# Turning queries by pairs of heads, a two-bank room for scores, and the root's small steps on GpSimd in a two-layer decoder trunk

## The chip, the cores and the metric

The kernel runs on one core of one Trainium2 chip. Its engines are TensorE (PE in the profile, with its weight loads as PEld), VectorE (DVE), ScalarE (ACT), GpSimd (POOL) and SyncE (SP), which issues DMAs. The metric is the device time of one execution in microseconds; lower is better.

## What is computed

A decoder trunk of two layers over 1024 tokens of width 1024 in f32. Layer 0 mixes tokens with a gated short convolution, layer 1 with attention in a sliding window of 128; each is followed by a SwiGLU channel mixer of width 2816. Every sub-layer has an RMS norm before it and a residual sum behind it. The change touches layer 1's attention alone:

```python
qkv = h @ w_qkv                        # 16 query heads, 4 key and 4 value heads, 64 wide
q = rmsnorm(q, q_gain); k = rmsnorm(k, k_gain)          # per head
scores = einsum(q, k) * scale + alibi  # blocks of 128 queries against 256 keys
scores = where(mask, scores, -inf)     # causal, distance below 128
p = softmax(concat([scores, sink]))[..., :-1]
out = einsum(p, v) @ w_o
```

## The kernel before

**Precision.** A f32 product is made of three fast matmuls: each operand is split into hi (the value rounded to the fast format, fp32r) and lo (the rest), and hi x hi, hi x lo and lo x hi are summed in PSUM. "Splitting" is therefore a pair of instructions everywhere: a copy to fp32r on ScalarE (…_hi) and a difference on VectorE or GpSimd (…_lo).

**The order.** From the first channel mixer on, the kernel is one long line written out by hand. `line.work(n, f)` appends n matmuls to TensorE's sequence and moves the plan's clock on by n x 0.2265 us; `at(t, f)` puts other work at a time of that clock. The times only set the order of instructions in each engine's queue; on the chip each engine runs its queue in order and waits by semaphores.

**Attention.** Work goes by m (16 half-tiles of queries: block m // 2 of 128 tokens, half m % 2 of the 16 heads) and by u (32 steps: a half-tile and one of its two key groups g, which share four query heads).

- `lead_in` makes keys, values and queries of the first blocks; then `unit(u)` is called for each step. In a step TensorE does the scores of u, the values of u-2, one piece of fill, the turns (128x128 transposes) of the probabilities of u-1, and five more pieces. A piece is three matmuls: of a coming query tile (`q_piece`), of coming keys and values (`kv_piece`), or, in the last steps, of the product with w_o (`tail_piece`).
- Queries: `q_square`, `q_sum` (sum of squares per head, and `mean_rows`), `q_guess` (Ln and Exp on ScalarE, for 1/sqrt), `q_newton` (one Newton step on VectorE), `q_scale` (q times that root, to SBUF). Then `q_hi` on ScalarE and `q_lo` on GpSimd split q in SBUF into [hi | lo] of each head, 128 columns a head; `q_turn` turns four heads for each g, and `q_keep` copies them out of PSUM. A turned block has hi of one head in partitions 0 to 63, lo in 64 to 127. Keys go the same way (`kv_square` to `kv_scale`, `key_turn`, `key_hi`, `key_lo`), with the key doubled along the partitions.
- Scores of a step lie in two PSUM banks of their own tags: `merge` puts the two halves of a window together, `bias` adds the distances (VectorE, once for each bank), `sink` (GpSimd) writes the sink's column beside them, `least` reduces, `exponents` (ScalarE), `inverse`, `normal` (GpSimd, division), `turn`, `turn_hi`, `turn_lo`, `select` (GpSimd, a triangular mask that splits the window), `values`, `o_copy`, `o_add`, `o_hi`, `o_lo` (GpSimd).
- PSUM has eight banks: P0 to P3 and acc0 to acc3. Query and key products use P0, P1 and P2, all turns of queries and nearly all of keys P3, probabilities' turns and values one acc bank each, scores the other two.
- In the last steps GpSimd also makes the lo part of w_o's first five tiles (line 1010) and issues stores of X (line 1064).

Of the kernel before, what the change touches and what calls it, by code (L numbers as in the profile page):

```python
# [15 lines left out]
P = 128  # L16
D = 1024
T = 1024
# [52 lines left out]
def trunk_kernel(ctx: ExitStack, tc: tile.TileContext, xT, small, table, w_in, w_out, w_kv, w_q, w_o, w_gu, w_dn, out):  # L71
# [13 lines left out]

    def bank(tag):
        uid[0] += 1
        if tag == "acc":
            tag = acc_tags[0]
            acc_tags.rotate(-1)  # L90
        return pm.tile([P, 512], F32, tag=tag, name=f"{tag}_{uid[0]}", bufs=1)
# [1405 lines left out]
    def attention_layer(line, mixer):  # L1497
# [3 lines left out]
        sc_tags = [acc_tags[0], acc_tags[1]]  # L1501
        pt_tag, pv_tag = acc_tags[2], acc_tags[3]
# [110 lines left out]

        def q_piece(m, k):
            c = slice((m % 2) * HALF, (m % 2 + 1) * HALF)
            piece(get_bank(q_ps, m, f"P{m // 2 % 2}" if m % 2 else "P2"), m // 2, k, lambda: (WQ[k][0][:, c], WQ[k][1][:, c]))


        def mean_rows(d, b, n):
            d["m"] = slot("at_m", (P, 8), bufs=2)[:, 0:n]  # L1620
            dve.tensor_scalar(d["m"], d["ss"], 1.0 / HD, tok["eps"][:, b : b + 1], ALU.mult, ALU.add)

        def log_rows(d, n):
            d["y"] = slot("at_y", (P, 8), bufs=2)[:, 0:n]
            act.activation(d["y"], d["m"], AF.Ln)

        def guess_rows(d):
# [49 lines left out]
        def kv_sum(b):  # L1677
            KV[b]["ss"] = slot("at_s", (P, 8), bufs=2)[:, 0:NKV]
            dve.tensor_reduce(KV[b]["ss"], KV[b]["sq"], mybir.AxisListType.X, ALU.add)
            mean_rows(KV[b], b, NKV)  # L1680

        def kv_guess(b):
            log_rows(KV[b], NKV)
            guess_rows(KV[b])

        def kv_scale(b):
            newton_rows(KV[b], NKV)
            y = KV[b]["y"].unsqueeze(2).to_broadcast([P, NKV, HD])
            for e in (0, 1):
                dve.tensor_tensor(kd_room()[:, :, e, :], kv_heads(b, 0), y, ALU.mult)  # L1690
# [8 lines left out]
        def key_turn(b, c):  # L1699
            ps = KT[b, c] = bank(pv_tag if b == 0 and c else "P3")  # L1700
            for g in (0, 1):
                k = kd_room()[:, 2 * c + g].rearrange("p e d -> p (e d)")
                pe.transpose(ps[:, g * P : (g + 1) * P], k, ident)
# [36 lines left out]
        def q_sum(m):  # L1740
            QC[m]["ss"] = slot("at_s", (P, 8), bufs=2)
            dve.tensor_reduce(QC[m]["ss"], QC[m]["x"], mybir.AxisListType.X, ALU.add)
            mean_rows(QC[m], m // 2, 8)

        def q_guess(m):
            log_rows(QC[m], 8)
            guess_rows(QC[m])
# [8 lines left out]
        def q_hi(m):  # L1756
            QC[m]["split"] = slot("G3", (P, 8, 2, HD))
            QC[m]["r"] = QC[m]["split"].bitcast(F32R)
            act.copy(QC[m]["r"][:, :, 0, :], QC[m]["q"])

        def q_lo(m):
            s = QC[m]["split"]
            pool.tensor_tensor(s[:, :, 1, :], QC[m]["q"], s[:, :, 0, :], ALU.subtract)

        def q_turn(m, g):
            ps = QC[m]["ps"] = bank(pt_tag if m == 0 and g else "P3")
            s = QC[m]["split"]
            for i in range(QUAD):
                pe.transpose(ps[:, i * P : (i + 1) * P], s[:, QUAD * g + i].rearrange("p e d -> p (e d)"), ident)

        def q_keep(m, g):
            if g == 0:
                Q[m] = slot(f"G{4 + m % 2}", (P, 2, QUAD * P), F32R)
            act.copy(Q[m][:, g], QC[m]["ps"])
# [16 lines left out]
        def scores(u):  # L1791
            b, c, g = parts(u)
            kz = key_rooms(c)[:, g]
            S[u] = {"ps": [bank(t) for t in sc_tags]}
            for i in range(QUAD):
                q = Q[2 * b + c][:, g, i * P : (i + 1) * P]
                ps = S[u]["ps"][i // 2][:, (i % 2) * 256 : (i % 2) * 256 + 256]
                for e in (0, 1):
                    k = kz[:, e].rearrange("p s j -> p (s j)")
                    if b == 0:  # L1800
                        ps, k = ps[:, 0:P], k[:, 0:P]
                    pe.matmul(ps, q, k, start=e == 0, stop=e == 1)  # L1802

        def logits(u, j):
            b, _, _ = parts(u)
            ps = S[u]["ps"][j].rearrange("p (i s c) -> p i s c", i=2, s=2)
            own_, prev = ps[:, :, b % 2, :], ps[:, :, (b + 1) % 2, :]
            return own_, prev

        def merge(u, j):  # L1810
            o, p = logits(u, j)
            dve.copy_predicated(p, own.unsqueeze(1).to_broadcast([P, 2, P]), o)

        def bias(u, j):
            b, c, g = parts(u)
            o, p = logits(u, j)
            h = 8 * c + QUAD * g + 2 * j
            e = e_room(u)
            dve.tensor_tensor(e[:, 2 * j : 2 * j + 2, 0:P], o if b == 0 else p, room["T"][:, h : h + 2, :], ALU.add)
# [102 lines left out]
        def lead_in(tail_part, tail_item):  # L1922
# [4 lines left out]
            for b in (0, 1):  # L1927
                d = t + (-0.6, 0.1)[b]
                at(d, kv_v_hi, b)
                at(d + 0.5, kv_v_lo, b)  # L1930
                at(d + 1.0, kv_square, b)
                at(d + 1.5, kv_sum, b)
                at(d + 2.2, kv_guess, b)
                at(d + (2.9, 8.2)[b], kv_scale, b)

            def quick(m, t):
                for d, f in (
                    (0.05, q_square),
                    (0.7, q_sum),
                    (1.6, q_guess),  # L1940
                    (2.3, q_newton),
                    (3.1, q_scale),
                    (3.9, q_hi),
                    (4.6, q_lo),
# [12 lines left out]
            def turn_query(m, g, t=None):  # L1957
                line.work(4 * small_turn, q_turn, m, g)
                at(line.end + 0.05 if t is None else t, q_keep, m, g)

            for k in range(NK):
                q_piece(1, k)
                if k in (1, 2):
                    turn_keys(0, k - 1, None, None)
            quick(1, line.end)
            q_piece(2, 0)
            q_piece(2, 1)
            turn_query(0, 0)
            q_piece(2, 2)
            q_piece(2, 3)  # L1970
            turn_query(0, 1)


# [27 lines left out]
            def unit(u, last):  # L2001
# [14 lines left out]
                if u < NU:  # L2016
                    line.work(8 * (small_mm + (0.12 if b else 0.0)), scores, u)
                    e = line.end
                    at(s + 0.3, sink, u)
                    for j in (0, 1):  # L2020
                        if b:
                            at(e + 0.05 + 0.85 * j, merge, u, j)
                        at(e + 0.5 + 0.85 * j, bias, u, j)
                    if b == 0:
                        at(e + 1.5, blank, u)
                    at(e + 1.8, least, u)
                    at(e + 2.65, exponents, u)
                    at(e + 4.75, inverse, u)
                    at(e + 5.0, normal, u)
                    if g == 0:  # L2030
                        kb = (b, 1) if c == 0 else (b + 1, 0)
                        if 0 < kb[0] < NB:
                            turn_keys(*kb, e + 0.3, e + 2.4)
                if 0 <= u - 2 < NU:
# [3 lines left out]
                    at(max(line.end + 0.7, s + 3.6), o_add, u - 2)  # L2038
                    if g == 1:
                        at(s + 6.95, o_hi, n - 1)  # L2040
                        at(s + 7.9, o_lo, n - 1)
                for _ in range(3 if u == NU else 1):
                    next_piece()
                if 0 <= u - 1 < NU:
                    line.work(4 * small_turn, turn, u - 1)
                    at(line.end + 0.05, turn_hi, u - 1)
                    at(max(line.end + 0.7, s + 4.2), turn_lo, u - 1)
                    if u - 1 >= 4:
                        at(line.end + 0.75, select, u - 1, 0)
                        at(max(line.end + 1.4, s + 4.95), select, u - 1, 1)  # L2050
# [4 lines left out]
                for i in range(5):  # L2055
                    next_piece()
                    if i == (1 if g == 0 else 0) and n + 1 < 16:
                        turn_query(n + 1, g, s + 5.8)
                if n + 2 < 16 and g == 0:
                    m = n + 2  # L2060
                    for d, f in (
                        (5.75, q_square),
                        (6.35, q_sum),
                        (7.2, q_guess),
                        (6.8 + 3.4, q_newton),
                        (6.8 + 5.2, q_scale),
                        (6.8 + 6.2, q_hi),
                        (6.8 + 7.3, q_lo),
                    ):
                        at(s + d, f, m)  # L2070
                if g == 1 and n < 12 and n % 2:
                    kb = n // 2 + 2
                    for d, f in (
                        (3.57, kv_v_hi),
                        (5.0, kv_v_lo),
                        (6.0, kv_square),
                        (6.5, kv_sum),
                        (7.2, kv_guess),
                        (6.8 + 3.5, kv_scale),
# [12 lines left out]
            for u in range(NU + 2):  # L2092
# [3 lines left out]
                unit(u, u == NU + 1)  # L2096
            while tails:
# [117 lines left out]
```

## Time and profile before

| | |
|---|---|
| median of 3 runs | 1919.74 us (1919.67 to 1920.07) |
| the profiled execution | 1919.71 us, its span 1918.0 us |
| granted TensorE clock | 1.000 |
| TensorE busy | 1906.7 us, 99% |
| VectorE, ScalarE, GpSimd busy | 1380.0, 855.6, 292.1 us |
| first to last scores of attention | 990.3 to 1209.7 us |

The span is from the first to the last instruction of the profiled execution; its own time has 1.7 us around that. Attention, with its lead-in, is about an eighth of the span, so 1% of the whole is some 8% of it.

### The profile page before, as it was taken

The numbers are of one execution on the slowest core, as the hardware profiler recorded it, in microseconds if no ns is written. First come the engines' busy times: TensorE is split into PE (matmuls) and PEld (weight loads), VectorE is DVE, ScalarE is ACT, GpSimd is POOL, SyncE is SP. The second block draws the span as 40 slices with busy tenths as digits, with TensorE's granted clock in tenths as the row PEclk, the third lists the DMA queues.
The fourth block names the chain that finished last, engine by engine and source line by source line (L and its number), as shares of the span: only waits on it lengthen the run. The fifth ranks groups of instructions, "written<-read, shape, count | busy, mean of one in ns | idle before, by whom it ended". The sixth has DMA issues, their size and how long they took to land.

```text
span 1918.0 us, 24702 instructions
## 1 busy us (share of the span) xinstructions
PE 1906.7 (99%) x8681; PEld 1579.5 (82%) x8681; DVE 1380.0 (72%) x2352; ACT 855.6 (45%) x1703; POOL 292.1 (15%) x462
## 2 busy tenths in 40 slices
PE   9999999999999999999999999999999999999999
PEld 8888888888888888888888887788888888888887
DVE  8997877867676767765768887678767776765543
ACT  5543444533333334444656766446333333344441
POOL 0000011011111111000015667500111111110000
PEclk9999999999999999999999999999999999999999
DMA  8522176145556447996710003433445555477563
GB/s 314 172 99 75 64 286 223 61 159 198 172 179 209 166 142 265 328 320 222 235 62 1 1 23 132 146 119 116 163 169 180 205 172 177 152 276 275 199 226 102
DMA packets 146765, 325.29 MB, mean 170 GB/s; under 512 B 14288, under 2 KB 54352, under 8 KB 146512
## 3 DMA queue, kind: packets, MB, share of 16 engines
q1 hardware_dynamic: 122592, 239.26, 36.9%
q0 software_dynamic: 23904, 84.42, 12.2%
q8 instruction: 68, 1.11, 0.2%
q14 instruction: 57, 0.47, 0.1%
q10 hardware_dynamic: 144, 0.03, 0.0%
HBM read 228.76 MB, written 94.90 MB: 169 GB/s over the span
## 4 chain that ended last, share of the span: by engine, by line
PE 92%; DVE 3%; issue 1%; POOL 1%; ACT 1%; DMA 1%; SPq 0%; POOLq 0%; DVEq 0%; ACTq 0%
PE acc L920 16%; PE acc L921 16%; PE acc L923 16%; PE P L920 9%; PE P L921 9%; PE P L923 9%; PE acc L1039 2%; PE acc L1037 2%; PE acc L1038 2%; PE P L1599 2%; PE P L1597 2%; PE P L1598 2%; PE acc L158 1%; PE acc L1802 1%; PE acc L1888 1%
## 5 line engine op out<-in xcount | busy, mean ns | idle before, releaser
L920 PE MATMUL acc<-XS,G 128*128 128x512 f32 x880 | 342.7, 389 | 0.0
L923 PE MATMUL acc<-XS,G 128*128 128x512 f32 x880 | 342.5, 389 | 0.0
L921 PE MATMUL acc<-XS,G 128*128 128x512 f32 x880 | 342.5, 389 | 0.0
L923 PEld LDWEIGHTS acc<-XS,G 128*128 128x128 f32 x880 | 165.2, 188 | 34.3
L920 PEld LDWEIGHTS acc<-XS,G 128*128 128x128 f32 x880 | 165.2, 188 | 34.3
L921 PEld LDWEIGHTS acc<-XS,G 128*128 128x128 f32 x880 | 165.2, 188 | 34.1
L920 PE MATMUL P<-A,G 128*128 128x512 f32 x476 | 185.3, 389 | 0.8 <-DVE G L1246 0.8
L923 PE MATMUL P<-A,G 128*128 128x512 f32 x476 | 185.3, 389 | 0.0
L921 PE MATMUL P<-A,G 128*128 128x512 f32 x476 | 185.2, 389 | 0.0
L920 PE MATMUL acc<-A,G 128*128 128x512 f32 x440 | 171.6, 390 | 0.0
L923 PE MATMUL acc<-A,G 128*128 128x512 f32 x440 | 171.3, 389 | 0.0
L921 PE MATMUL acc<-A,G 128*128 128x512 f32 x440 | 171.2, 389 | 0.0
L860 DVE TENSOR_TENSOR G<-WL,G 128x512 fp32r<-128x512 f32 x168 | 114.8, 684 | 53.1 <-ACT G L859 53.1
L859 ACT CAST G<-WR 128x512 fp32r<-128x512 f32 (+1 forms) x200 | 121.0, 605 | 60.4 <-PE acc L923 26.2
L860 DVE TENSOR_TENSOR G<-WR,G 128x512 fp32r<-128x512 f32 (+1 forms) x200 | 133.1, 666 | 11.1 <-ACT G L859 10.7
L859 ACT CAST G<-WH 128x512 fp32r<-128x512 f32 (+1 forms) x158 | 94.9, 601 | 79.7 <-PE acc L923 42.2
L1208 ACT ACTIVATE G<-G 128x512 f32<-128x512 f32 x88 | 55.8, 634 | 162.1 <-DVE G L1279 157.9
L920 PE MATMUL P<-XS,G 128*128 128x512 f32 x316 | 123.1, 390 | 0.1
L921 PE MATMUL P<-XS,G 128*128 128x512 f32 x316 | 123.0, 389 | 0.0
L923 PE MATMUL P<-XS,G 128*128 128x512 f32 x316 | 123.0, 389 | 0.0
L859 ACT CAST G<-WL 128x512 fp32r<-128x512 f32 x168 | 103.5, 616 | 37.0 <-DVE WL L803 33.2
L860 DVE TENSOR_TENSOR G<-WH,G 128x512 fp32r<-128x512 f32 (+1 forms) x158 | 104.3, 660 | 7.5 <-ACT G L859 7.2
(305 smaller groups left out, 3843.2 us busy)
## 6 DMA issues: line engine op xcount, KB each, us to landing
G<-h SPq DMA_DIRECT2D x70, 512.0 KB, 5.4
h<-X POOLq DMA_DIRECT2D x44, 512.0 KB, 5.0
X<-in_w_dn SPq DMA_DIRECT2D x80, 256.0 KB, 3.4
s<-X POOLq DMA_DIRECT2D x40, 512.0 KB, 4.7
WR<-in_w_gu SPq DMA_DIRECT2D x36, 512.0 KB, 6.1
WH<-in_w_gu SPq DMA_DIRECT2D x36, 512.0 KB, 6.5
h<-X POOLq DMA_DIRECT2D x66, 256.0 KB, 4.1
WR<-s SPq DMA_DIRECT2D x54, 256.0 KB, 3.4
```

The source lines that it names most:

```text
L859: lambda: act.copy(out_hi, raw),
L860: lambda: lo_eng.tensor_tensor(out_lo, raw, plain(out_hi), ALU.subtract),
L920: pe.matmul(ps, w[:, 0, c], x[:, 0, :], start=start and e == 0, stop=False, skip_group_check=True)
L921: pe.matmul(ps, w[:, 0, c], x[:, 1, :], start=False, stop=False, skip_group_check=True)
L923: pe.matmul(ps, w[:, 1, c], x[:, 0, :], start=False, stop=last, skip_group_check=True)
L1037: pe.matmul(ps, hi[:, kc], xs[:, 0, c], start=k == 0, stop=False, skip_group_check=True)
L1038: pe.matmul(ps, hi[:, kc], xs[:, 1, c], start=False, stop=False, skip_group_check=True)
L1039: pe.matmul(ps, lo[:, kc], xs[:, 0, c], start=False, stop=k == n_op - 1, skip_group_check=True)
L1208: state["silu"] = act.activation(x, x, AF.Silu)
L1597: pe.matmul(ps, x[:, 0, t], hi, start=k == 0, stop=False)
L1598: pe.matmul(ps, x[:, 0, t], lo, start=False, stop=False)
L1599: pe.matmul(ps, x[:, 1, t], hi, start=False, stop=k == NK - 1)
```

## The change

- Queries are turned unsplit: `q_turn` turns four f32 blocks of 128x128, two heads in each, in one group for a half-tile. The split follows behind the turn, out of PSUM: `q_hi` (ScalarE) copies the upper or the lower 64 partitions as hi, `q_lo` (VectorE) writes the rest into the other 64 partitions of the same room. `q_keep` and the split in SBUF are gone; the room Q[m] is now indexed by the head's place in its pair.
- The turns of keys and of queries of a step follow each other, after the probabilities' turns, in steps with g = 0; keys turn into the bank of the query product that has just been scaled, in place of P3.
- The scores of a step lie in one tile of two banks, `twin`, in a PSUM pool of its own that is closed and opened again around attention; `merge` and `bias` are one instruction each, over 512 columns.
- `mean_rows` and `newton_rows` go from VectorE to GpSimd (one and four instructions, where there were one and three); ScalarE's Ln reads the sum of squares itself, with scale and bias. The key's second copy is a ScalarE copy in place of a second product on VectorE.
- `sink` of a step is issued in the step before, and most written times are moved.

```diff
+    def open_ends():        # a PSUM pool of its own for acc0, acc1 or twin
+        if "stack" in ends:
+            ends["stack"].close()
+        ...
-        sc_tags = [acc_tags[0], acc_tags[1]]
-        pt_tag, pv_tag = acc_tags[2], acc_tags[3]
+        pt_tag, pv_tag = "acc2", "acc3"
...
         def mean_rows(d, b, n):
-            dve.tensor_scalar(d["m"], d["ss"], 1.0 / HD, tok["eps"][:, b : b + 1], ALU.mult, ALU.add)
+            pool.tensor_scalar(d["m"], d["ss"], 1.0 / HD, tok["eps"][:, b : b + 1], ALU.mult, ALU.add)
...
-            act.activation(d["y"], d["m"], AF.Ln)
+            act.activation(d["y"], d["ss"], AF.Ln, scale=1.0 / HD, bias=tok["eps"][:, b : b + 1])
...
         def newton_rows(d, n):
-            dve.tensor_tensor(t, d["y"], d["y"], ALU.mult)
-            dve.scalar_tensor_tensor(t, t, -0.5, d["m"], ALU.mult, ALU.mult)
-            dve.scalar_tensor_tensor(d["y"], t, 1.5, d["y"], ALU.add, ALU.mult)
+            pool.tensor_tensor(t, d["y"], d["y"], ALU.mult)
+            pool.tensor_tensor(t, t, d["m"], ALU.mult)
+            pool.tensor_scalar(t, t, -0.5, 1.5, ALU.mult, ALU.add)
+            pool.tensor_tensor(d["y"], d["y"], t, ALU.mult)
...
-            ps = KT[b, c] = bank(pv_tag if b == 0 and c else "P3")
+            ps = KT[b, c] = bank(q_tag(2 * b + c) if b else ("P3", pv_tag)[c])
...
-        def q_hi(m):
-            QC[m]["split"] = slot("G3", (P, 8, 2, HD))
-            ...
-        def q_turn(m, g):
-            ps = QC[m]["ps"] = bank(pt_tag if m == 0 and g else "P3")
-            ...
+        def q_turn(m):
+            ps = QC[m]["ps"] = bank("P3")
             for i in range(QUAD):
-                pe.transpose(ps[:, i * P : (i + 1) * P], s[:, QUAD * g + i].rearrange("p e d -> p (e d)"), ident)
+                q = QC[m]["q"][:, 2 * i : 2 * i + 2].rearrange("p e d -> p (e d)")
+                pe.transpose(ps[:, i * P : (i + 1) * P], q, ident)
+        def q_hi(m, e):
+            rows = slice(e * HD, (e + 1) * HD)
+            act.copy(Q[m][rows, e], QC[m]["ps"][rows])
+        def q_lo(m, e):
+            rows, rest = slice(e * HD, (e + 1) * HD), slice((1 - e) * HD, (2 - e) * HD)
+            dve.tensor_tensor(Q[m][rest, e], QC[m]["ps"][rows], plain(Q[m])[rows, e], ALU.subtract)
...
         def scores(u):
+            twin = ends["pool"].tile([P, 2, 512], F32, tag="twin", name=f"twin_{u}", bufs=1)
...
-        def merge(u, j):
-            o, p = logits(u, j)
-            dve.copy_predicated(p, own.unsqueeze(1).to_broadcast([P, 2, P]), o)
+        def merge(u):
+            o, p = logits(u)
+            dve.copy_predicated(p, own.unsqueeze(1).to_broadcast([P, QUAD, P]), o)
...
-                    at(s + 0.3, sink, u)
+                    if u + 1 < NU:
+                        at(s + 3.6, sink, u + 1)
...
+                if g == 0:
+                    kb = (b, 1) if c == 0 else (b + 1, 0)
+                    if 0 < kb[0] < NB:
+                        turn_keys(*kb, s + 3.7, s + 4.7)
+                    if n + 1 < 16:
+                        turn_query(n + 1, (s + 6.2, s + 6.8), (s + 6.9, s + 6.5 + 3.2))
-                for i in range(5):
+                for _ in range(5):
                     next_piece()
-                    if i == (1 if g == 0 else 0) and n + 1 < 16:
-                        turn_query(n + 1, g, s + 5.8)
```

More of the change, by code (lines that the diff above doesn't have):

```diff
@@ L84, in pair_slot @@
         return slot(tag, (P, 2, D), F32R)
+    ends = {}
+    def open_ends():
+        if "stack" in ends:
+            ends["stack"].close()
+        ends["stack"] = ExitStack()
+        uid[0] += 1
+        ends["pool"] = ends["stack"].enter_context(
+            tc.tile_pool(name=f"pe{uid[0]}", bufs=1, space=bass.MemoryType.PSUM)
+        )
+        return ends["pool"]
+    open_ends()
+    ctx.callback(lambda: ends["stack"].close())
     def bank(tag):
@@ L90, in bank @@
             acc_tags.rotate(-1)
+        if tag in ("acc0", "acc1"):
+            return ends["pool"].tile([P, 512], F32, tag=tag, name=f"{tag}_{uid[0]}", bufs=1)
         return pm.tile([P, 512], F32, tag=tag, name=f"{tag}_{uid[0]}", bufs=1)
@@ L1679, in kv_sum, with kv_mean, kv_newton, kv_twice @@
             dve.tensor_reduce(KV[b]["ss"], KV[b]["sq"], mybir.AxisListType.X, ALU.add)
+        def kv_mean(b):
             mean_rows(KV[b], b, NKV)
         def kv_guess(b):
-            log_rows(KV[b], NKV)
-            guess_rows(KV[b])
+            guess_rows(KV[b], b, NKV)
+        def kv_newton(b):
+            newton_rows(KV[b], NKV)
         def kv_scale(b):
-            newton_rows(KV[b], NKV)
             y = KV[b]["y"].unsqueeze(2).to_broadcast([P, NKV, HD])
-            for e in (0, 1):
-                dve.tensor_tensor(kd_room()[:, :, e, :], kv_heads(b, 0), y, ALU.mult)
+            dve.tensor_tensor(kd_room()[:, :, 0, :], kv_heads(b, 0), y, ALU.mult)
+        def kv_twice(b):
+            act.copy(kd_room()[:, :, 1, :], kd_room()[:, :, 0, :])
         def key_rooms(c):
@@ L1932, in lead_in @@
                 at(d + 1.5, kv_sum, b)
+                at(d + 2.0, kv_mean, b)
                 at(d + 2.2, kv_guess, b)
[L1934 removed]
+                at(d + 2.7, kv_newton, b)
+                at(d + (3.7, 8.2)[b], kv_scale, b)
+                at(d + (4.2, 8.7)[b], kv_twice, b)
             def quick(m, t):
@@ L1939, in quick @@
                     (0.7, q_sum),
-                    (1.6, q_guess),
-                    (2.3, q_newton),
+                    (1.4, q_mean),
+                    (1.5, q_guess),
+                    (2.0, q_newton),
                     (3.1, q_scale),
-                    (3.9, q_hi),
-                    (4.6, q_lo),
                 ):
@@ L1955, in turn_keys, with turn_query @@
                 at(t_lo if t_lo is not None else line.end + 0.5, key_lo, b, c)
-            def turn_query(m, g, t=None):
-                line.work(4 * small_turn, q_turn, m, g)
-                at(line.end + 0.05 if t is None else t, q_keep, m, g)
+            def turn_query(m, t_hi, t_lo):
+                line.work(4 * small_turn, q_turn, m)
+                for e in (0, 1):
+                    at(t_hi[e], q_hi, m, e)
+                    at(t_lo[e], q_lo, m, e)
             for k in range(NK):
                 q_piece(1, k)
-                if k in (1, 2):
-                    turn_keys(0, k - 1, None, None)
+                if k == 2:
+                    turn_keys(0, 0, None, None)
+                    turn_keys(0, 1, None, None)
             quick(1, line.end)
[L1966 to L1971, printed above, removed]
+            t = line.end
+            turn_query(0, (t + 0.55, t + 1.15), (t + 1.2, t + 1.9))
+            for k in range(4):
+                q_piece(2, k)
             fill = []
@@ L2018, in unit @@
                     e = line.end
-                    at(s + 0.3, sink, u)
[L2020 to L2023, printed above, removed]
-                    if b == 0:
[L2025 to L2033, printed above, removed]
+                    if u == 0:
+                        at(s - 2.0, sink, 0)
+                    if u + 1 < NU:
+                        at(s + 3.6, sink, u + 1)
+                    if b:
+                        at(e + 0.05, merge, u)
+                    at(e + 0.75, bias, u)
+                    if b == 0:
+                        at(e + 1.0, blank, u)
+                    at(e + 1.5, least, u)
+                    at(e + 3.0, exponents, u)
+                    at(e + 5.1, inverse, u)
+                    at(e + 5.2, normal, u)
                 if 0 <= u - 2 < NU:
@@ L2037, in unit @@
                     at(line.end + 0.05, o_copy, u - 2)
-                    at(max(line.end + 0.7, s + 3.6), o_add, u - 2)
+                    at(max(line.end + 0.7, s + 3.3), o_add, u - 2)
                     if g == 1:
-                        at(s + 6.95, o_hi, n - 1)
-                        at(s + 7.9, o_lo, n - 1)
+                        at(s + 6.7, o_hi, n - 1)
+                        at(s + 7.6, o_lo, n - 1)
                 for _ in range(3 if u == NU else 1):
@@ L2046, in unit @@
                     at(line.end + 0.05, turn_hi, u - 1)
-                    at(max(line.end + 0.7, s + 4.2), turn_lo, u - 1)
+                    at(max(line.end + 0.7, s + 4.0), turn_lo, u - 1)
                     if u - 1 >= 4:
                         at(line.end + 0.75, select, u - 1, 0)
-                        at(max(line.end + 1.4, s + 4.95), select, u - 1, 1)
+                        at(max(line.end + 1.4, s + 4.75), select, u - 1, 1)
                 if u >= NU:
@@ L2061, in unit @@
                     for d, f in (
[L2062 to L2068, printed above, removed]
+                        (5.9, q_square),
+                        (6.6, q_sum),
+                        (7.3, q_mean),
+                        (7.35, q_guess),
+                        (8.0, q_newton),
+                        (6.5 + 5.0, q_scale),
                     ):
@@ L2096, in lead_in @@
                 unit(u, u == NU + 1)
+            at(line.end - 3.0, open_ends)
             while tails:
```

59 lines of the change are left out of this document (28 added, 31 removed).

## The prediction

> **What bounds the kernel now.** I read the front page first: the span, the busy shares, and the chain of work that ended last.
>
> ```profile
> span 1918.0 us, 24702 instructions
> PE 1906.7 (99%) x8681; PEld 1579.5 (82%) x8681; DVE 1380.0 (72%) x2352; ACT 855.6 (45%) x1703; POOL 292.1 (15%) x462
> PE 92%; DVE 3%; issue 1%; POOL 1%; ACT 1%; DMA 1%; SPq 0%; POOLq 0%; DVEq 0%; ACTq 0%
> ```
>
> TensorE is busy all the time and carries 92% of the chain. A busy share can still hide bubbles, because the ends of matmuls are modelled; so I go on to the starts of TensorE's instructions, in the timeline, over one step of attention.
>
> ```profile
> 1106.81 1.12 PE L1802 MATMUL acc<-G,G 128*128 128x256 f32 x8
> ...
> 1109.38 0.60 PE L1853 MATMUL acc<-cst,G 128*128 128x128 f32 x4
> ...
> 1110.05 0.40 PE L1598 MATMUL P<-WH,XS 128*128 128x512 f32 x1
> 1110.29 0.39 PE L1599 MATMUL P<-WH,XS 128*128 128x512 f32 x1
> 1110.52 0.60 PE L1769 MATMUL P<-cst,G 128*128 128x128 f32 x4
> 1110.88 0.48 PE L1597 MATMUL P<-A,XS 128*128 128x512 f32 x1
> 1111.19 0.39 PE L1598 MATMUL P<-A,XS 128*128 128x512 f32 x1
> ...
> 1113.71 0.52 PE L1802 MATMUL acc<-G,G 128*128 128x256 f32 x3
> ```
>
> Columns are start, time, line, tiles and count. A step runs from scores to scores, 1106.81 to 1113.71: 6.9 us. Matmuls of 512 columns start 0.23 us apart (1110.29 to 1110.52) though each is shown as 0.39 long, so nothing but their number sets this stretch. The group of four query turns (L1769) lies between 1110.52 and 1111.19; that 0.67 also holds one matmul of 0.23. A group therefore costs 0.44 us of TensorE, with no extra for switching. Next, the windows, columns PE, PEld, DVE, ACT, POOL: four steps in the middle of attention, and the end of it.
>
> ```profile
> 1053.00:1081.00 28.00, 28.00 (x158) 23.84 (x156) 24.08 (x54) 19.68 (x67) 18.28 (x30) 1.00 0.01 1
> 1193.00:1226.00 33.00, 32.11 (x161) 25.82 (x160) 24.52 (x39) 19.26 (x57) 25.25 (x40) 1.00 0.27 97
> ```
>
> In the middle TensorE has no hole and VectorE is next, at 86%; at the end GpSimd is up to 77%, and TensorE has holes. The clock is 1.00 in both. Last, the waits of TensorE's weight loads. All of these lie inside attention: who waited for whom, total us, times, longest.
>
> ```profile
> PEld acc L1853 <- POOL G L1847: 3.7, 7, 0.9
> PEld P L1769 <- issue: 2.2, 2, 1.3
> PEld P L1769 <- POOL XS L1919: 1.9, 3, 1.2
> PEld acc L1888 <- POOL G L1869: 1.5, 3, 0.8
> PEld P L1769 <- POOL G L1763: 1.3, 3, 0.6
> PEld P L1703 <- ACT G L1774: 1.2, 1, 1.2
> ```
>
> They sum to 11.8 us in 19 waits. While a load waits, the matmul ahead of it still runs for 0.23, so 11.8 - 19 x 0.23 = 7.4 us of TensorE's time is lost to waits in attention. That is the second thing which the change can move.
>
> **Part 1: half of the query turns go.** Before, every half-tile of queries (16 of them) is split first and its eight [hi|lo] blocks are turned in two groups; after, four f32 blocks of two heads are turned in one group.
>
> ```profile
> L1769 PEld LDWEIGHTS P<-cst,G x124: 137/141/145, 987.7 to 1199.2; 128*128 128x128 f32 x124
> L1769 PE MATMUL P<-cst,G x124: 270/272/330, 987.7 to 1199.3; 128*128 128x128 f32 x124
> ```
>
> These 124 and the 4 into an accumulator bank make 128 turns; 64 stay. They are f32 before and after, with the same shape, so their price stays. 16 groups x 0.44 = 7.0 us, directly on the engine that sets the end. The scores keep their eight matmuls per step: the two heads of a pair lie in two halves of the partitions, and each half-tile Q holds hi in one half and lo in the other, so a matmul still contracts 128 rows. The key turns and the turns of probabilities keep their number and only move; by the group above, place costs nothing.
>
> **Part 2: the work around it moves.** Prices, from the groups by line in 1053 to 1165 us (busy us, mean ns of one, idle before), and for L1621 from the whole trace (minimum/median/maximum ns):
>
> ```profile
> L1774 ACT CAST G<-P 128x512 fp32r<-128x512 f32 x16 | 9.2, 575 | 0.0
> L1902 ACT COPY s<-acc 64x512 f32<-64x512 f32 x8 | 4.6, 580 | 3.7 <-PE acc L1888 3.4
> L1906 DVE TENSOR_TENSOR s<-acc,s 64x512 f32<-64x512 f32 x8 | 5.5, 694 | 0.3
> L1763 POOL TENSOR_TENSOR G<-s,G 128x512 f32<-128x512 f32 x8 | 10.4, 1295 | 0.0
> L1824 POOL COPY G<-cst 128x4 f32<-128x4 f32 x15 | 2.9, 190 | 0.0
> L1919 POOL TENSOR_TENSOR XS<-s,XS 128x128 fp32r<-128x128 f32 x16 | 6.9, 463 | 0.0
> L1819 DVE TENSOR_TENSOR G<-acc,A 128x256 f32<-128x256 f32 x32 | 13.6, 425 | 8.4 <-POOL G L1824 7.1
> L1812 DVE COPY_PREDICATED acc<-cst,acc 128x256 f32<-128x256 int32 x31 | 13.0, 421 | 1.8 <-PE acc L1802 1.6
> L1621 DVE TENSOR_SCALAR at_m<-at_s,eps_r x24: 230/544/1048, 976.8 to 1178.0; 128x8 f32<-128x8 f32 x16, 128x4 f32<-128x4 f32 x8
> ```
>
> I count per four steps, in which two half-tiles of queries and, up to two thirds of the way, one block of keys go through.
> - ScalarE loses two q_hi (at 0.58, the size of L1774) and four q_keep (0.575). It gains four q_hi of 64x512 (0.58, as L1902) and kv_twice, no dearer than 0.58. 19.7 - 1.2 + at most 0.6 is about 19 of 27 us: not the bound.
> - VectorE loses three means (0.54), nine Newton instructions (0.23 each, the minimum of the mean, which has as few columns), and one key scaling (0.42). Eight merges and eight biases of 0.42 become four and four of 512 columns; 0.69 as L1906 is the nearest row, so 6.8 becomes 5.5. It gains four q_lo (0.69). Together -1.6 - 2.1 - 0.4 - 1.3 + 2.8 = -2.6: 24.1 becomes 21.5. Cover grows.
> - GpSimd loses two q_lo (1.295) and gains 15 small steps. No such step is in the trace. It costs at least the 0.19 of the copy of 4 columns and at most the 0.463 of two operands of 128; I take 0.29, near the copy because 8 columns are nearest to it, with some for the hand-over from step to step. 18.3 - 2.6 + 15 x 0.29 = 20.0, by the ends 18.5 and 22.6, of 27.1 us that four steps then last (28.0 less two groups of turns). Hidden in the middle; if that cover were gone, every us above 27.1 would be paid in each four steps.
> - The root's chain gets longer by the hand-overs, but q_scale is written some 4 us after the guess, and the turn that needs it comes in the next pair of steps. Queued behind the Newton steps on GpSimd are its next sink, selects and normal; they are due 2 us or more after it by the written times. No DMA is added or moved; GpSimd's stores of xres come later than any root step.
> - The two-bank room makes the first merge wait for all eight score matmuls instead of four, 0.5 us later, and scores of the next step for one bias instead of two; that bias ends some 4 us before them. I cost it at nothing.
>
> **Part 3: which waits go.** Three of the rows of waits (L1769 on L1919, on L1763, and on issue) and L1703 on L1774 belong to the query's and key's turns: q_lo queued on GpSimd behind o_lo, and one bank, P3, handed to and fro between key and query turns. After the change q_lo isn't ahead of a turn at all, and key turns go to the query's own free bank. 2.2 + 1.9 + 1.3 + 1.2 = 6.6 us in 9 waits, less 9 x 0.23: 4.5 us that I take as gone. The other two rows (L1853, L1888) are the probabilities' turns and values, which wait for normal and select on GpSimd; 5.2 us in 10 waits, 2.9 lost, most of it at the end of the stage. One cause shows there:
>
> ```profile
> 1180.37 1.03 POOL L1847 TENSOR_TENSOR G<-G,at_d 128x512 f32<-128x512 f32 x1
> 1181.37 0.72 POOL L1010 TENSOR_TENSOR WL<-WR,WH 128x256 fp32r<-128x256 f32 x1
> 1182.04 0.18 POOL L1824 COPY G<-cst 128x4 f32<-128x4 f32 x1
> ...
> 1182.26 0.43 DVE L1819 TENSOR_TENSOR G<-acc,A 128x256 f32<-128x256 f32 x1 [3.36 <-POOL G L1824]
> ```
>
> VectorE stood 3.36 us before the bias, for a copy of 0.18 (the sink) that was queued behind the previous step's normal and a piece of w_o's split. So normal, sink, bias, exponents and the next normal form a ring with other work in it. The change issues a step's sink in the step before, ahead of that normal, and the ring is cut. But GpSimd remains 77% busy there, so I take only half of the 2.9 us as gone: 1.4.
>
> Late next are the banks. A key turn of the odd half now uses a bank that the fifth piece of the same step writes: three pieces (9 x 0.23 = 2.1 us) and the query's turns (0.44) later, 2.5 us in which ScalarE must do key_hi and VectorE key_lo, behind the split of the probabilities.
>
> ```profile
> L1707 ACT ACTIVATE G<-P,qkg 128x256 fp32r<-128x256 f32 x8 | 3.7, 462 | 0.0
> L1712 DVE SCALAR_TENSOR_TENSOR G<-P,qkg,G 128x256 fp32r<-128x256 f32 x8 | 3.8, 475 | 0.0
> ```
>
> The two take 0.94, and turn_hi and turn_lo ahead of them about 0.58 + 0.69 by the like rows above: 2.2 of 2.5 in a row, with some overlap. It occurs seven times. I put 0.1 each, 0.7 in all, between nothing and 1.0 each.
>
> **Sum.** The profiled execution took 1919.71 us, its span 1918.0 and 1.7 around it; the median of the runs is 1919.74, so the sum holds for it too. 1919.7 - 7.0 (turns) - 4.5 (waits at the turns of queries and keys) - 1.4 (normal and select) + 0.7 (bank of the key turn) = 1907.5 us.
>
> **The rivals.**
> - *The turns go, the waits stay.* The tail of attention is set by GpSimd, and a wait that is lifted from a query's turn is met again at the next probability turn. For it: GpSimd's 25.25 of 33 us at the end. Against: the largest waits are those of P3, which has a new owner. Time: 1919.7 - 7.0 = 1912.7.
> - *The new bank exchange eats the gain.* Seven exchanges at 1.0 us, and all old waits stay: 1919.7 - 7.0 + 7.0 = 1919.7, no change. For it: 2.2 us of work in a gap of 2.5. Against: VectorE has 2.6 us less to do in four steps.
> - *GpSimd becomes the bound*, the case of slower. It is at 18.3 - 2.6 = 15.7 us per four steps without the new steps; from (28.0 - 15.7) / 15 = 0.82 us a step on, four steps last longer than before. The trace gives a way: the 8-column mean on VectorE takes from 230 to 1048 ns, so a small instruction can stand behind a large one of the other engine. A step of 0.29 behind one VectorE instruction of 0.69 is 0.98: 15.7 + 14.7 = 30.4, 2.4 us more than now, in some seven groups of four steps: 1919.7 + 17 = 1937. Against: nearly all of VectorE's large instructions in attention have one operand in PSUM (acc or P in the rows), and GpSimd's copy of 4 columns is a steady 190 ns. The Trainium skill, "SBUF — State Buffer", section "SBUF: two separate sides", says that VectorE and GpSimd hold one port pair exclusively for a whole instruction, VectorE when both its inputs are in SBUF or in a two-port mode. By that rule the spread of the mean is that lock, and it would be rarer after the change, since the small SBUF instructions leave VectorE. The trace agrees as far as the 230 to 1048 ns go. The skill also says, in "GPSIMD Engine Reference", section "4.1 Engine selection", that elementwise arithmetic belongs on VectorE, GpSimd being about twice as slow; by that rule a step would be an estimated 0.46 (twice the mean's 0.23), GpSimd 22.6 of 27.1, and the sum the same; no row of a small GpSimd instruction with two operands shows it.
>
> **How the numbers follow.** The forecast has 63%: its waits are from 0 left (1919.7 - 7.0 - 7.4 = 1905.3) to half left, 1909 to 1910. Turns alone 24%, at 1912.7 and up to 1916 with a few exchanges. The bank exchange 7%, between 1916 and 1923. GpSimd as the bound 6%. The range goes from 1904.5 to 1915. A measurement of this kernel can tell about 0.2%, 3.8 us, from no change. Faster: 63 + 24 + 1; the same: 6; slower: 6.
>
> **What would show it.** The query's turns: 64 in place of 128, each group still 0.44 from start to start, and scores to scores 6.7 us on average in the middle. Waits of the loads: none on P3, less than 3 us in all on normal and select. VectorE's waits for the sink: gone. GpSimd's small steps: 0.2 to 0.46 each. Wrong it would be if these steps took 0.8 and more, if TensorE had a hole of the same size in every step, or if a kv piece stood regularly for key_lo.

## The result, and the profile after

The changed kernel takes 1904.72 us (median, 1904.29 to 1905.08), the kernel before 1919.7 us: a ratio of 0.9922, 95% interval 0.9904 to 0.9939. That is 15.0 us less, where 12.2 were forecast. The whole difference lies in attention: from the first piece to the last values TensorE needs 262.6 us before (nearer a seventh of the span than an eighth) and 247.5 us after, and what follows the last values takes 692.6 us in both traces.

The front page of the changed kernel's profiled execution (1904.92 us):

```profile
span 1903.1 us, 24503 instructions
PE 1896.5 (100%) x8617; PEld 1574.7 (83%) x8617; DVE 1363.1 (72%) x2220; ACT 852.7 (45%) x1695; POOL 297.9 (16%) x566
PE 97%; DVE 2%; issue 1%; ACT 0%; DMA 0%; DVEq 0%; ACTq 0%
```

64 matmuls of TensorE are gone, and the chain now lies on TensorE for 97%, where it was 92%. One step with turns of queries and keys, from scores (L1827) to scores, in the timeline:

```profile
1039.72 1.12 PE L1827 MATMUL twin<-G,G 128*128 128x256 f32 x8
...
1042.29 0.60 PE L1876 MATMUL acc<-cst,G 128*128 128x128 f32 x4
1042.73 0.38 PE L1726 MATMUL P<-cst,G 128*128 128x128 f32 x2
1042.95 0.60 PE L1784 MATMUL P<-cst,s 128*128 128x128 f32 x4
1043.31 0.48 PE L1613 MATMUL P<-X,XS 128*128 128x512 f32 x1
1043.62 0.40 PE L1614 MATMUL P<-X,XS 128*128 128x512 f32 x1
...
1046.84 0.40 PE L1827 MATMUL twin<-G,G 128*128 128x256 f32 x2
```

The ten turns stand in one row: 1042.29 to 1043.62 is 1.33, of which one matmul is 0.23; 1.10 for ten, the 0.11 a turn that the groups of four cost before. This step takes 7.1 us and the next, without query or key turns, 6.4; four steps from 1046.84 on take 27.12 us, as forecast. The windows of the middle and of the end of attention (columns as before), and the waits of weight loads in attention (955 to 1260 us):

```profile
1053.00:1081.00 28.00, 28.00 (x156) 24.04 (x156) 21.79 (x39) 19.35 (x67) 19.97 (x45) 1.00 0.00 1
1178.00:1211.00 33.00, 32.98 (x170) 27.57 (x170) 24.30 (x37) 21.05 (x61) 26.53 (x44) 1.00 0.27 98
```

```profile
PEld acc L1876 <- POOL G L1870: 1.2, 4, 0.4
PEld twin L1827 <- issue: 0.5, 1, 0.5
PEld P L1613 <- DVE G L1735: 0.2, 1, 0.2
```

At the end of attention TensorE's holes are closed, though GpSimd is no emptier than before (26.53 of 33 us against 25.25). VectorE's waits for the sink, 18.7 us in 17 waits before, are no longer among its rows. Of 11.8 us of weight-load idle in the rows shown before, 1.9 us in six waits are left; less 0.23 for each, 0.5 us of TensorE. (Two rows of 0.3 us each, at the first scores and at the values, were not among the rows shown before.) GpSimd's small steps, from the groups by line in attention (us busy, mean ns, idle before):

```profile
L1640 POOL TENSOR_SCALAR at_m<-at_s,eps_r 128x8 f32<-128x8 f32 (+1 forms) x24 | 6.6, 274 | 121.4 <-DVE at_s L1697 112.2 <-DVE at_s L1765 7.7
L1650 POOL TENSOR_TENSOR at_t<-at_t,at_m 128x8 f32<-128x8 f32 (+1 forms) x24 | 4.9, 205 | 1.9
```

### The profile page after: what moved, and what is told of

The parts are those of the page before. It is cut to its first block, busy times and chain, and to the rows that moved or that the text cites. A ratio compares the mean times of both kernels' runs of the same rounds, so it can differ in the third digit from the quotient of the medians.

```text
span 1903.1 us, 24503 instructions
## 1 busy us (share of the span) xinstructions
PE 1896.5 (100%) x8617; PEld 1574.7 (83%) x8617; DVE 1363.1 (72%) x2220; ACT 852.7 (45%) x1695; POOL 297.9 (16%) x566
## 4 chain that ended last, share of the span: by engine, by line
PE 97%; DVE 2%; issue 1%; ACT 0%; DMA 0%; DVEq 0%; ACTq 0%
PE acc L937 16%; PE acc L940 16%; PE acc L938 16%; PE P L937 9%; PE P L938 9%; PE P L940 9%; PE P L1613 2%; PE P L1615 2%; PE P L1614 2%; PE acc L1056 2%; PE acc L1054 2%; PE acc L1055 2%; PE twin L1827 2%; PE acc L1911 1%; PE acc L175 1%; PE P L1054 1%
## 5 line engine op out<-in xcount | busy, mean ns | idle before, releaser
L877 DVE TENSOR_TENSOR G<-WR,G 128x512 fp32r<-128x512 f32 (+1 forms) x200 | 133.2, 666 | 12.2 <-ACT G L876 11.9
```

The source lines that it names most:

```text
L877: lambda: lo_eng.tensor_tensor(out_lo, raw, plain(out_hi), ALU.subtract),
```

## The experiments

My theory was: 7 us are the turns; the rest are waits, the larger part of them at bank P3 and at q_lo, the smaller at a ring through the sink. The rivals were that the waits only move, and that the covered work (roots, merges) isn't covered. Each experiment changes one thing in the changed kernel or in the kernel before. Beside each of them the kernel before took 1919.98 to 1920.1 us on the same chip; the changed kernel's 1904.72 us stand beside 1919.7, so a difference from it is good to some 0.4 us.

**The turns alone.** In `q_turn` of the changed kernel:

```diff
-            for i in range(QUAD):
+            for i in list(range(QUAD)) * 2:
```

> The changed kernel with each query's group of four turns issued twice into the same bank (the second writes the same values). If the turns lie directly on the path, 16 more groups at 0.44 us give 7.0 us: 1904.7 + 7.0 = 1911.7 us, and attention (first piece to last values, 247.5 us in the changed kernel) lasts 254.5. If the gain came from the waits alone and the turns lay in holes, it stays within 1 us of 1904.7.

Measured 1911.91 us (1911.63 to 1912.19), 7.2 more than the changed kernel; attention lasts 254.5 us. The 64 additional turns cost 7.0 us there, 0.109 each. The turns lay on the path in full.

**The sink, in the kernel before.**

```diff
-                    at(s + 0.3, sink, u)
+                    if u == 0:
+                        at(s - 2.0, sink, 0)
+                    if u + 1 < NU:
+                        at(s + 3.6, sink, u + 1)
```

> The kernel before with one thing of the change: each step's sink is issued in the step before, ahead of that step's normal. If the ring through the sink made the late waits, 1.5 to 3 us go: 1916.7 to 1918.2, and the waits of the probabilities' turns on normal (3.7 us of weight-load idle) fall to under 1.5. If the waits have another cause (GpSimd's load, P3), it stays at 1919.7.

1915.99 us (1915.63 to 1916.43) against 1920.0, a ratio of 0.9979 (0.9970 to 0.9988): 4.0 us, more than I had expected, and at another place. The weight loads' waits of this kernel:

```profile
PEld acc L1853 <- POOL G L1847: 3.2, 6, 0.9
PEld P L1769 <- POOL G L1763: 1.2, 3, 0.6
PEld P L1769 <- POOL XS L1919: 1.2, 1, 1.2
PEld acc L1888 <- POOL G L1869: 0.8, 3, 0.4
PEld P L1769 <- issue: 0.3, 1, 0.3
```

The row of the probabilities' turns (L1853) has hardly fallen, from 3.7 to 3.2, where I had looked for under 1.5. What fell are the rows of the query and key turns: L1769 on issue from 2.2 to 0.3, on L1919 from 1.9 to 1.2, and L1703 on L1774 from 1.2 to nothing.

**The bank, in the kernel before.**

```diff
-            ps = KT[b, c] = bank(pv_tag if b == 0 and c else "P3")
+            m = 2 * b + c
+            tag = f"P{m // 2 % 2}" if m % 2 else "P2"
+            ps = KT[b, c] = bank(tag if b else ("P3", pv_tag)[c])
```

> The kernel before with one thing of the change: key turns of blocks 1 to 7 go to the bank of the query product that has just been scaled, and P3 is left to the query's turns. If the bank handed to and fro made the waits there, the waits of key turn on q_keep and of query turn on key_lo (some 1.1 + 1.0 us, and part of those shown as issue and o_lo) go: 1916 to 1917.5 us. If q_lo's place behind o_lo in GpSimd's queue was the cause, 1919 to 1919.7.

1920.47 us against 1920.0, a ratio of 1.0001 (0.9992 to 1.0010): nothing. Attention itself is 0.5 us shorter, and 1.2 us are lost after it; why, I did not follow.

```profile
PEld acc L1855 <- POOL G L1849: 5.3, 11, 0.9
PEld acc L1890 <- POOL G L1871: 2.9, 8, 0.8
PEld P L1771 <- POOL G L1765: 1.7, 4, 0.6
PEld P L1705 <- DVE s L1756: 1.3, 2, 0.7
PEld acc L1890 <- DVE G L1867: 1.1, 3, 0.5
```

The waits at P3 (issue, L1919) are gone here too, but the time was met again at the turns of probabilities (L1855, from 3.7 to 5.3) and at the values (L1890, from 1.8 in two rows to 4.0 in two). VectorE still stands for the sink, by its own waits:

```profile
DVE G L1821 <- POOL G L1826: 20.0, 16, 3.4
```

So for the late waits the bank was where TensorE stood, not why. VectorE works its queue in order; while it stood at bias (L1819) for the sink, key_lo (L1712) stood behind it, and P3 was handed over late. In the kernel before, VectorE and the query's turns that wait for it:

```profile
1190.24 0.43 DVE L1819 TENSOR_TENSOR G<-acc,A 128x256 f32<-128x256 f32 x1 [2.51 <-POOL G L1824]
...
1192.11 0.47 DVE L1712 SCALAR_TENSOR_TENSOR G<-P,qkg,G 128x256 fp32r<-128x256 f32 x1
```

```profile
1192.72 0.63 PE L1769 MATMUL P<-cst,G 128*128 128x128 f32 x4 [0.90 <-DVE G L1712]
```

One wait at P3 is of another kind: the 1.2 us of load idle at 1020 (L1769 on L1919). VectorE does not stand for the sink there; the wait stays with the early sink and goes only with the other bank.

**Both, in the kernel before.** The two edits above together.

> The kernel before with the early sink (alone 1916.0 against 1920.0) and the key turns off P3 (alone 1920.5 against 1920.0) together. If P3 was a cause that only the ring through the sink hid, some 1 us more goes: 1914.5 to 1915.3. If the waits at P3 were VectorE standing for the sink, and the bank no cause of its own, it equals the early sink alone: 1916 within 0.5.

1916.81 us (1916.59 to 1917.75) against 1919.98, a ratio of 0.9983 (0.9975 to 0.9992). Attention is 258.4 us against 258.7 with the sink alone, and 1.2 us are lost after it, as in the run of the bank alone. The wait at 1020 is gone, and a key turn waits 0.7 us for q_scale shortly before that place instead. The bank had a cost of its own of 0.3 us at most in that order of work.

**The sink, in the changed kernel.** The reverse of the edit above.

> The changed kernel with the sink's column written in its own step, as before, behind the previous step's normal in GpSimd's queue. If the ring normal, sink, bias, exponents, normal made the waits at the end of attention, VectorE waits for the sink again, and 1.5 to 3 us of the waits of the probabilities' turns come back: 1906 to 1908 us. If the rest of the new order already gave enough room, it stays at 1904.7, within 0.5.

1907.22 us (1906.80 to 1907.44), 2.5 more: the time that the first reading gave, but only in part at its place. The probabilities' turns wait 1.8 us where they waited 1.2. VectorE stands for the sink again, and TensorE behind it, most of it where a bank is handed over by key_lo (L1735):

```profile
PEld acc L1876 <- POOL G L1870: 1.8, 4, 0.7
PEld P L1054 <- DVE G L1735: 1.6, 2, 1.1
```

```profile
DVE G L1842 <- POOL G L1847: 4.8, 6, 1.9
```

**The key turns' bank, in the changed kernel.**

```diff
-            ps = KT[b, c] = bank(q_tag(2 * b + c) if b else ("P3", pv_tag)[c])
+            ps = KT[b, c] = bank("P3" if b or not c else pv_tag)
```

> The changed kernel with the key turns back in bank P3, which the query's turns directly behind them use too. If the bank was a cause of the waits at the turns, each of 14 query turns now stands for key_hi and key_lo behind turn_hi and turn_lo, some 1 to 1.7 us each: 1919 to 1929 us, with the weight loads of the query's turn waiting on key_lo. If only q_lo's place in GpSimd's queue was the cause, and the bank none, it stays below 1906.

1953.36 us (1952.17 to 1955.4), 48.6 more, twice what I had expected as the most. All 14 query turns that follow a key turn wait for key_lo, as the weight loads and as the matmuls show it:

```profile
PEld P L1784 <- DVE G L1735: 30.5, 14, 2.6
PE P L1784 <- DVE G L1735: 27.1, 14, 2.3
```

With the turns of a step in one row, the other bank is needed. The waits are 30.5 us, though, not 48; where the rest is, the windows around one of them show (the wait, then what follows; after the busy times come the granted clock, the DMA share and GB/s):

```profile
1053.40:1055.40 2.00, 0.15 (x2) 0.00 (x0) 1.94 (x5) 1.97 (x8) 1.75 (x8) 1.00 0.00 0
1055.40:1058.00 2.60, 2.57 (x9) 2.18 (x10) 0.48 (x2) 0.52 (x4) 1.55 (x2) 0.55 0.02 6
1058.00:1062.00 4.00, 4.00 (x21) 3.40 (x20) 0.90 (x2) 2.17 (x5) 0.28 (x1) 0.87 0.00 0
```

After this wait of 2 us the granted clock is 0.55. In attention there are 11 such stretches of 3.41 us at half the clock behind the 14 waits. They lose 11 x 3.41 x 0.5 = 18.8 us; with 27.1 us of idle matmuls that is 45.9 of the 47.5 us by which attention is longer. Most of the waits are paid a second time.

**The roots on VectorE, in the changed kernel.** `mean_rows` and `newton_rows` as before, at the written times of the change.

```diff
-            pool.tensor_scalar(d["m"], d["ss"], ...)
+            dve.tensor_scalar(d["m"], d["ss"], ...)
...
-            pool.tensor_tensor(t, d["y"], d["y"], ALU.mult)
-            ...                                        # four steps on GpSimd
+            dve.tensor_tensor(t, d["y"], d["y"], ALU.mult)
+            dve.scalar_tensor_tensor(t, t, -0.5, d["m"], ALU.mult, ALU.mult)
+            dve.scalar_tensor_tensor(d["y"], t, 1.5, d["y"], ALU.add, ALU.mult)
```

> The changed kernel with the mean and the Newton step on VectorE again (one and three instructions), at the same written times. If GpSimd's part in the change was only to relieve engines that are not the bound, TensorE sees nothing: 1904.7 to 1906 us, VectorE 24 to 25 of 27 us per four steps in the middle instead of 21.8, GpSimd some 16.5. If moving them was what removed waits, 1908 us or more.

1914.06 us (1913.71 to 1914.57): 9.3 more. The second reading holds. Most of it is one place, which comes six times. VectorE's timeline in this kernel up to a key_lo (L1734), and TensorE's instruction that waits for it:

```profile
1043.07 0.34 DVE L1640 TENSOR_SCALAR at_m<-at_s,eps_r 128x4 f32<-128x4 f32 x1
1043.33 0.68 DVE L1835 COPY_PREDICATED twin<-cst,twin 128x512 f32<-128x512 int32 x1
1043.92 0.32 DVE L1649 TENSOR_TENSOR at_t<-at_y 128x4 f32<-128x4 f32 x1
1044.28 0.38 DVE L1650 SCALAR_TENSOR_TENSOR at_t<-at_t,at_m 128x4 f32<-128x4 f32 x1
1044.69 0.38 DVE L1651 SCALAR_TENSOR_TENSOR at_y<-at_t,at_y 128x4 f32<-128x4 f32 x1
1044.99 0.68 DVE L1841 TENSOR_TENSOR G<-twin,A 128x512 f32<-128x512 f32 x1
...
1047.76 0.47 DVE L1734 SCALAR_TENSOR_TENSOR G<-P,qkg,G 128x256 fp32r<-128x256 f32 x1
```

```profile
1048.29 0.50 PE L1613 MATMUL P<-WR,XS 128*128 128x512 f32 x1 [0.84 <-DVE G L1734]
```

One small instruction stands ahead of merge (L1835) and three between merge and bias (L1841), 0.3 to 0.4 us each; key_lo ends at 1048.2, and the kv piece that writes key_lo's bank stood for it. In the changed kernel the same two lie so:

```profile
1044.46 0.48 DVE L1735 SCALAR_TENSOR_TENSOR G<-P,qkg,G 128x256 fp32r<-128x256 f32 x1
```

```profile
1045.25 0.19 PEld L1613 LDWEIGHTS P<-WR,XS 128*128 128x128 f32 x1
```

key_lo ends at 1044.94 and the load comes at 1045.25: a margin of 0.3 us. The 9.3 us are the price of the changed order without the move of the roots, and no share of the 15.0: in the kernel before the roots were on VectorE too, with 7.4 us of waits in all.

**The same, with the key's Newton step written later** (7.6 becomes 6.5 + 5.1, behind key_lo).

> The changed kernel with the roots on VectorE (1914.1 with the written times kept), and the key's Newton step written 4 us later, behind key_lo in VectorE's queue. If the 9 us were key_lo's place behind those steps, the waits of the kv piece on key_lo (6.3 us of weight-load idle, five times) go: 1905 to 1907.5 us, with VectorE as busy as in that run. If VectorE's load as such is what costs, 1911 us or more.

1909.07 us (1908.82 to 1909.18): 5.0 of the 9.3 are back, between the two expectations. The waits on key_lo are five again, but 1.9 us in all where they were 6.3:

```profile
PEld acc L1875 <- POOL G L1869: 2.8, 5, 0.9
PEld P L1613 <- DVE G L1734: 1.9, 5, 0.4
```

More than half was the place in the queue. I put the rest down to the other small instructions on VectorE, of which the key's mean is still ahead of key_lo; that is not shown, for I have not divided it further.

**Merge and bias by banks.** Two instructions of 256 columns each in place of one, in the same room.

```diff
-            dve.copy_predicated(p, own.unsqueeze(1).to_broadcast([P, QUAD, P]), o)
+            for j in (0, 1):
+                o, p = (x[:, 2 * j : 2 * j + 2] for x in logits(u))
+                dve.copy_predicated(p, own.unsqueeze(1).to_broadcast([P, 2, P]), o)
```

> The changed kernel with merge and bias as two instructions of 256 columns each on the same room of two banks. VectorE has about 1.3 us more in four steps of 27. If VectorE is covered by TensorE, no change: 1904.7 within 0.5. If the shorter way from scores to normal is what removed the late waits, 1906 to 1908, with TensorE's weight loads waiting for normal.

1905.95 us (1905.61 to 1906.63), 1.2 more, attention 0.7 us longer. Loads wait 1.6 us for normal in place of 1.2, and 0.5 for key_lo in place of 0.2. The wide merge is a small part of the gain.

**Turns one by one.** The same 64 turns, with a piece between each of the four of a half-tile; three of the four instructions of the split that follows are written some 0.5 us later (not shown here).

```diff
-                    if n + 1 < 16:
-                        turn_query(n + 1, (s + 6.2, s + 6.8), (s + 6.9, s + 6.5 + 3.2))
-                for _ in range(5):
+                for i in range(5):
                     next_piece()
+                    if g == 0 and i < QUAD and n + 1 < 16:
+                        line.work(small_turn, q_turn, n + 1, (i,))
```

> The changed kernel with the same 64 query turns, but in 15 of the 16 half-tiles each of the four turns stands alone, with a piece of fill between them. In both traces matmuls start 227 ns apart in a long run and 231 to 236 ns for about ten matmuls behind a group of turns. If each interruption costs that, 60 new ones at 0.03 to 0.05 us give 1.8 to 3 us: 1906.5 to 1907.7. If a turn costs the same wherever it stands (as the prediction had it), 1904.7 within 0.5.

1908.69 us (1908.10 to 1908.94), 4.0 more, but mostly not for the reason given. A turn that stands alone:

```profile
1099.67 0.39 PE L1615 MATMUL P<-X,XS 128*128 128x512 f32 x1
1099.90 0.27 PE L1786 MATMUL P<-cst,s 128*128 128x128 f32 x1
1099.92 0.47 PE L1613 MATMUL P<-X,XS 128*128 128x512 f32 x1
1100.24 0.39 PE L1614 MATMUL P<-X,XS 128*128 128x512 f32 x1
```

```profile
PEld acc L1878 <- POOL G L1872: 3.7, 5, 1.2
```

From 1099.67 to 1100.24 are 0.57; less two matmuls of 0.227 it is 0.116 for one turn (median of 60: 118 ns), against 0.111 in a group. 60 x 0.007 is 0.4 us. The rest appears as waits, above all of the probabilities' turns, 3.7 us for normal instead of 1.2. That the later split makes them is likely, but not shown. A row of turns is worth little to TensorE itself.

**One more piece ahead of the first scores.**

```diff
-            for k in range(4):
+            for k in range(5):
                 q_piece(2, k)
...
-                    first += [(q_piece, n + 2, k) for k in range(4, 8)]
+                    first += [(q_piece, n + 2, k) for k in range(4 if n else 5, 8)]
```

> The changed kernel with five instead of four pieces of the third query tile ahead of the first scores. The first scores' wait for q_lo (0.5 us of weight-load idle) goes: attention 0.3 to 0.5 us shorter, 1904.2 to 1904.5 us. If the wait only moves (to the next query's turn, which then comes as early against its scaling), no change in the length of attention.

1904.51 us (1904.24 to 1904.85): by time not to be told from the changed kernel. In the trace attention is 0.44 us shorter, 247.07 against 247.51, and the first scores' wait is gone. It is the lowest of all that I ran.

## Why the prediction was right, and where its sum was off

- **The turns, 7.0 us**: right, on the path and in size (7.0 us for the same number added).
- **The waits at the turns of queries and keys, 4.5 us**: right in size, for they are gone; wrong in cause for the larger part. The step put them down to q_lo's place and to the owner of P3. The bank alone brought nothing, the early sink alone brought 4.0 us, and most of it at these very turns: their rows fell from 6.6 us of load idle to 2.7. The row of a wait named the bank that TensorE stood at; the ring through the sink, which the same part of the prediction shows, stood behind it. That the size came out right is thus partly luck. Of the 2.7 us that the sink left, 2.4 fit the step: 1.2 us on q_lo (L1763), and the 1.2 us at 1020 that went with the bank.
- **Normal and select, 1.4 of 2.9 us**: too small. 1.2 us of load idle are left in four waits, 0.3 of TensorE, so 2.6 went. Not all of it was the ring: with the early sink alone these two rows fell only from 5.2 to 4.0 us. "GpSimd remains 77% busy" was no reason to keep half: it is 80% busy now (26.53 of 33) and is hardly waited for. That leaves the order in its queue, which the sink shows for a part (1.8 us on normal with the late sink, 1.2 with the early one); what removed the rest, q_lo's departure or the other new times, is not shown.
- **The new bank exchange, +0.7**: nothing; one wait of 0.2. The margin is 0.3 us, though, and the rival that I gave 7% is what happens when VectorE is given 1.4 us more ahead of key_lo, as in the kernel with the roots there.
- **Work at no cost under TensorE**: the shares were right (for the four steps from 1046.84 VectorE 21.5 forecast, 21.5 measured; ScalarE 19 and 19.3; GpSimd 20.0 and 19.2, a step of 0.20 to 0.27 for the 0.29 taken). But the step "cover grows" missed what the move of the roots was worth: 9.3 us at these written times. With VectorE at 23.4 of 28 us, TensorE still stood.
- **GpSimd as the bound**: far off. Each Newton step on GpSimd took 194 to 210 ns and the mean 264 to 279, without a long one among 24 of each. In the kernel with the roots on VectorE the like instructions were mostly shorter there, a median of 0.17 us for a Newton step, but up to 0.68, and 0.32 to 0.38 in the timeline above. So the move did not make the steps cheaper; it took them out of VectorE's queue.

The miss of 2.8 us is thus: normal and select 1.2, the bank 0.7, and 0.9 left over. By the waits and the turns alone I get 7.0 + 7.4 - 0.5 = 13.9 of 15.0 us. The starts of the matmuls, which need no modelled ends, bear this out. Take as a hole whatever a pair of successive matmuls starts more than 0.03 us further apart than the median of pairs of the same kinds (those right behind a turn taken apart). The holes of attention then sum to 8.4 us before and 1.3 us after, so 7.1 went, where 7.4 - 0.5 is 6.9. The 1.0 us left over lies in differences below 0.03 us a pair. Fewer interruptions by turns would be a small part of that, at 7 ns each; what the rest is I leave open.

## What to carry to other kernels

Where one engine is busy without a hole, count what it no longer has to issue; here that price, 7.0 us, came back in full. For the waits beside it, follow the releaser one step further than the row: an engine that works in order makes everything behind its first wait late, and the wait that shows on the bounding engine is at some bank that it was to release. A share of busy time tells neither: ask at each hand-over how many tenths of a microsecond are left, and what stands ahead of the releasing instruction in its queue.

## What the runs showed of the hardware

A wait of TensorE can cost twice. In the kernel with key turns in P3, TensorE is without work for about 2 us once in two steps; in 11 of 14 cases the clock is then granted at half for 3.41 us (0.55 and 0.87 are its means in the windows above), and matmuls that start 0.23 apart start 0.43 apart. 27.1 us of idle time, by the waits of its matmuls, became 47.5 us more of attention. Three such waits, of 1.9 to 2.3 us, were not followed by it. Waits of up to 1.0 us, in the kernel before, left the clock at 1.00 (the mean over its span). The Trainium skill, "TensorE: Matmul & The Clock Gate", Part 1, says that the gate goes to half after an idle window of some 3.4 us. Here the matmuls stood idle for 1.9 to 2.3 us. But each wait lies in a row of ten turns, so that 3.3 to 4.1 us pass from the start of the last other matmul to the start of the next one. Whether the turns count as work for the clock, and with it whether 2 us of idleness are enough, no run here shows.
